# Four more pairs of projections in the seven-product part, and weights split ahead in the attention

## The chip, the cores and the metric

The kernel runs on one core of one Trainium2 chip. The metric is the device time of one execution in microseconds (us); of several executions the median is given. Work is spread over engines that run side by side, each through its own list of instructions in order: TensorE (PE, matmuls into PSUM), VectorE (DVE), ScalarE (ACT), GpSimd (POOL) and SyncE (SP), which here only issues DMAs. POOL issues some DMAs too. A DMA is issued when the instructions ahead of it in its queue are through and the buffers that it needs are free.

## The reference

Two layers on 512 latent and 256 context tokens of width 1024, in float32. The first mixes a long convolution (Hyena) and grouped-query attention; the second is an mLSTM with 8 heads, run over the tokens forwards and backwards. For the second layer the input `h` is projected to queries and keys of 128 columns a head and to values `v`, gates `o` and `z` of 256 columns a head:

```python
q, k, v, o, z, gates = _split(h @ w_in, ODD_SPLITS)
...
h = (h_f + h_b).transpose(0, 2, 1, 3).reshape(Bn, n, ML_WIDTH).astype(o.dtype) * jax.nn.sigmoid(o)
h = rms_norm(h.reshape(Bn, n, ML_HEADS, ML_V), head_norm.reshape(ML_HEADS, ML_V)).reshape(Bn, n, ML_WIDTH)
return (h * jax.nn.silu(z)) @ w_out
```

Keys and values are wanted for all 768 tokens, since the state starts from the context; queries, `o` and `z` for the 512 latent tokens alone.

## The kernel before

**Precision.** Every float32 operand is split into a rounded half `hi` and the rest `lo`: a copy with conversion on ACT and a subtract on DVE (`split`, line 1005). A product is then three matmuls, hi x hi, hi x lo and lo x hi (`mm3`, line 1015). A projection of one tile of 128 tokens on 256 columns goes over 8 blocks of the inner dimension, so it takes 24 matmuls of 256 columns (`proj_tok`, line 1202). The activations lie in SBUF as `hTh` and `hTl`.

**Weights.** `load_w` (line 1030) loads a slice of 1024 x 256 weights in two halves of 512 KB into one of three raw buffers `wr` (SP's queue) and splits each into `wh0`/`wl0` or `wh1`/`wl1`, two sets that take turns.

**Stages**, each recorded whole and then issued in an order that is written out in lists (`ORDERS`), which fix the sequence on every engine; `SLOTS` says which buffer each use of a tile gets:

- `start` and `hy`: norms, then the convolution in eight rounds `j`.
- `att`: 24 blocks `n` (8 heads by 3 groups of 256 queries). Scores (two PSUM tiles `s`), their maximum on DVE, the exponential on ACT into `hdh`/`hdl`, the scaling on DVE, transposes on PE, splits into `PTh`/`PTl`, and the products with the values (`values`, line 2006). Between them stand projections for the next heads. Behind block 19 the output projection begins, whose sums go into the tile `yacc0`; until then `yacc0` is unused. The query norms take a small power on POOL (`rstd`, line 1076; tile `rq`).
- `out0`: the rest of the first layer's output, and the second layer's input.
- `l1a`: values of head 0, the mLSTM's gate terms, keys and queries of head 0, and gates `o` and `z` of heads 0 to 6 by seven products.
- `l1b`: for each head `h` the recurrence in both directions (scores with `E`, the state `C` with its halves `Ch` and `Cl`, the sums `num`), interleaved with keys, queries and six value tiles of head `h + 1` (`heads`, line 2527). With the last head the work that stands between is `o` and `z` of head 7.
- `out1`: the second layer's output. Its first 96 matmuls already stand at the end of `l1b`.

**Seven products.** Two projections of the 512 latent tokens, `o` and `z` of a head, are taken as one product of 2 x 2 blocks: 256 tokens by 512 inner rows, times 512 inner rows by 256 columns of `o` or of `z`. A scheme of Strassen's kind needs seven block products instead of eight, each 24 matmuls: 168 for a pair. The sums of activations (`D1`, `F5`, `F6`, `F3`) are made once. The four sums of weight blocks for each pair are made in DRAM during the convolution: `oz_sums` (line 1635) issues, in each of the eight rounds, one copy (SP's queue) or one accumulating DMA (POOL's queue) for each of seven pairs, 512 KB each, into `osum`. In `gates_oz` (line 2484) a pair loads seven blocks of 512 KB (three through `wr`, four through the two buffers `ch`), splits them, and combines the products on DVE in seven operations of 512 columns; `o` and `z` then go through ACT and to DRAM, from where `l1b` loads them.

All instructions go through one helper, so each row of the profile has the same line, L1000; they are told apart by the tiles that they write and read.

Of the kernel before, what the change touches and what calls it, by code (L numbers as in the profile page):

```python
# [2777 lines left out]
```

## Time and profile before

| | |
|---|---|
| three executions | 1489.63, 1490.12, 1491.56 us, median 1490.12 |
| profiled execution | 1491.61 us, span 1489.8 us |
| granted TensorE clock, mean | 0.997 |
| busy share of PE, DVE, ACT, POOL | 98%, 70%, 51%, 6% |
| stage `hy`, to about 395 us | PE without a break |
| stage `att`, about 425 to 742 us | DVE about 69%, ACT about 48% busy between 395 and 715 us |
| stage `l1a`, about 870 to 1045 us | DVE 73%, ACT 61% busy |
| stage `l1b`, 1045 to 1390 us | DVE 75%, ACT 68% busy |

The stages run into each other by some us. A row of groups reads: line, engine, operation, tile written <- tiles read, shapes, count | busy us, mean ns of one | idle time of the engine ahead of them and what ended it. A row of a tile gives the least, middle and longest duration in ns, the first and the last start in us, and the shapes. A row of waits reads: who <- for whom, us in total, times, longest us. A row of DMA issues gives the queue, the count, the size of one and the median us from issue to landing. POOLq and SPq are the queues of POOL and SP.

### The profile page before, as it was taken

What the parts mean: (1) busy time and instruction counts of PE and PEld (TensorE: products, weight loads), DVE (VectorE), ACT (ScalarE), POOL (GpSimd) and SP (SyncE); (2) the same over time, 40 slices, a digit from 0 to 9 for tenths busy, and PEclk for the clock granted to TensorE, in tenths of its full rate; (3) what the DMA queues carried; (4) which work ended last, traced back from release to release, by engine and by line L of the source; (5) the groups of instructions that cost most, each with busy time, mean ns of one, the idle gap of its engine ahead of it and who ended that gap; (6) DMA issues with size and microseconds to landing.
All of it is one profiled execution on the core that took longest, in us unless ns stands there. A gap on an engine that the chain in (4) does not pass through costs nothing. (4 is left out here: it accounts for less than half of the span.)

```text
span 1489.8 us, 25927 instructions
## 1 busy us (share of the span) xinstructions
PE 1457.7 (98%) x10362; PEld 1339.3 (90%) x10362; DVE 1037.1 (70%) x1927; ACT 766.3 (51%) x1577; POOL 82.5 (6%) x125
## 2 busy tenths in 40 slices
...
GB/s 378 221 140 144 146 162 131 147 140 183 76 100 43 54 96 54 82 117 114 164 222 68 134 123 155 203 267 198 156 117 97 113 62 86 124 88 140 153 205 123
DMA packets 57353, 205.79 MB, mean 138 GB/s; under 512 B 7003, under 2 KB 8539, under 8 KB 54448
## 3 DMA queue, kind: packets, MB, share of 16 engines
...
q14 instruction: 40, 0.33, 0.1%
...
## 5 line engine op out<-in xcount | busy, mean ns | idle before, releaser
L1000 PE MATMUL pj<-wh,hTh 128*128 128x256 f32 (+2 forms) x1200 | 340.6, 290 | 0.8 <-ACT qjunk L1000 0.4
L1000 PE MATMUL pj<-wl,hTh 128*128 128x256 f32 (+2 forms) x1200 | 337.4, 287 | 0.3 <-DVE wl L1000 0.3
L1000 PE MATMUL pj<-wh,hTl 128*128 128x256 f32 (+2 forms) x1200 | 336.7, 288 | 0.0
L1000 PE MATMUL pj<-hTh,wh 128*128 128x512 f32 (+1 forms) x832 | 286.8, 346 | 0.4 <-DVE vl L1000 0.3
L1000 PE MATMUL pj<-hTl,wh 128*128 128x512 f32 (+1 forms) x832 | 285.4, 344 | 0.4 <-DVE hTl L1000 0.4
L1000 PE MATMUL pj<-hTh,wl 128*128 128x512 f32 (+1 forms) x832 | 285.5, 345 | 0.0
L1000 PEld LDWEIGHTS pj<-wh,hTh 128*128 128x128 f32 x1200 | 224.3, 189 | 6.2 <-issue 2.7
L1000 PEld LDWEIGHTS pj<-wl,hTh 128*128 128x128 f32 x1200 | 225.0, 189 | 2.9 <-DVE wl L1000 0.5
L1000 PEld LDWEIGHTS pj<-wh,hTl 128*128 128x128 f32 x1200 | 223.9, 189 | 3.5 <-issue 1.5
L1000 DVE TENSOR_TENSOR wl<-wr,wh 128x1024 fp32r<-128x1024 f32 (+1 forms) x142 | 171.4, 1213 | 63.9 <-ACT wh L1000 63.9
L1000 ACT CAST wh<-wr 128x1024 fp32r<-128x1024 f32 (+1 forms) x142 | 146.7, 1043 | 83.4 <-PE pj L1000 55.8
L1000 PEld LDWEIGHTS pj<-hTh,wh 128*128 128x128 f32 x832 | 156.6, 189 | 18.5 <-DVE vl L1000 1.1
L1000 PEld LDWEIGHTS pj<-hTl,wh 128*128 128x128 f32 x832 | 156.8, 189 | 17.9 <-DVE hTl L1000 0.7
L1000 PEld LDWEIGHTS pj<-hTh,wl 128*128 128x128 f32 x832 | 156.4, 188 | 18.0 <-DVE wl L1000 0.3
L1000 DVE TENSOR_TENSOR PTl<-pj,PTh 128x384 fp32r<-128x384 f32 (+1 forms) x80 | 41.1, 526 | 18.8 <-ACT PTh L1000 18.4
L1000 ACT CAST PTh<-pj 128x384 fp32r<-128x384 f32 (+1 forms) x80 | 35.6, 459 | 30.5 <-PE pj L1000 29.8
L1000 DVE TENSOR_TENSOR wl<-ch,wh 128x1024 fp32r<-128x1024 f32 x28 | 34.2, 1221 | 24.5 <-ACT wh L1000 24.4
L1000 DVE TENSOR_REDUCE mx<-s 128x1 f32<-128x768 f32 (+1 forms) x48 | 37.2, 775 | 11.4 <-PE s L1000 11.2
L1000 PE MATMUL pm<-Rh,dfa 128*128 128x256 f32 (+1 forms) x192 | 45.0, 305 | 0.0
L1000 DVE TENSOR_TENSOR med<-big 128x512 f32<-128x512 f32 (+1 forms) x48 | 40.4, 864 | 5.0 <-ACT big L1000 4.8
L1000 PE MATMUL s<-dfa,qTh 128*128 128x256 f32 (+1 forms) x160 | 42.8, 338 | 0.7 <-ACT hdh L1000 0.6
L1000 DVE SCALAR_TENSOR_TENSOR C<-C,apb,pj 128x258 f32<-128x258 f32 x64 | 30.8, 481 | 16.5 <-PE pj L1000 11.8
...
## 6 DMA issues: line engine op xcount, KB each, us to landing
wr<-in_e_w_in SPq DMA_DIRECT2D x52, 512.0 KB, 5.3
wr<-in_o_w_in SPq DMA_DIRECT2D x50, 512.0 KB, 5.2
o_sums<-in_o_w_in POOLq DMA_DIRECT2D x28, 512.0 KB, 7.1
ch<-o_sums SPq DMA_DIRECT2D x21, 512.0 KB, 4.9
wh<-in_w_mod SPq DMA_DIRECT2D x10, 1024.0 KB, 7.3
wl<-in_w_mod SPq DMA_DIRECT2D x9, 1024.0 KB, 7.6
wr<-in_e_w_out SPq DMA_DIRECT2D x16, 512.0 KB, 4.5
wr<-in_o_w_out SPq DMA_DIRECT2D x16, 512.0 KB, 4.6
```

Source lines behind the costliest of these rows:

```text
L1000: x = fn(*a, **k)
```

## The change

1. The seven-product part takes eleven pairs instead of seven. The four new ones stand first: values of heads 1 and 2, of 3 and 4, of 5 and 6, and gate `o` of head 7 with values of head 7. Only latent tokens are done that way. The values are split there and both halves go to DRAM; `l1b` loads them into `vh` and `vl` and projects only the two context tiles of each head. The sums in DRAM grow accordingly, from 7 to 11 DMAs a round.
2. In the attention, behind each block's product with the values, up to three pieces of weights are split ahead: keys and queries of heads 2 to 7 and values of heads 1 to 7, 52 pieces of 128 x 512 (256 KB). A piece is loaded on POOL's queue into one of three places in `yacc0`, cast on ACT, subtracted on DVE, and both halves are stored to DRAM on POOL's queue.
3. In `l1b` these weights are loaded as ready halves straight into `wh`/`wl`, 1 MB each, on SP's queue.
4. `out_gate` of head 7 is gone from `l1b`.
5. The lists of order and buffers are new for `att` and the stages behind it. In `hy` the sequence is the same but for the DMAs added.

```diff
-    osum = nc.dram_tensor("o_sums", [7, 4, P, 4, 256], F32).ap()
+    PAIRS = [(5, 9), (13, 17), (21, 25), (30, 29)] + [(4 * h + 2, 4 * h + 3) for h in range(7)]
+    osum = nc.dram_tensor("o_sums", [len(PAIRS), 4, P, 4, 256], F32).ap()
+    def pair_blocks(n):
+        a, b = (ow[x] for x in PAIRS[n])
+        return a[:, 0:4], b[:, 0:4], a[:, 4:8], b[:, 4:8]
...
+    wsd = nc.dram_tensor("w_scratch", [8, 2, 2, P, KT, 256], F32).ap()
+    ahead = [(h, t, k) for h in range(1, 8) for t in range(2) for k in range(0, KT, 2)][4:]
+    begun = []
+    def split_ahead():
+        if begun:
+            h, t, k, hi, lo = begun.pop()
+            S.copy(hi, f(lo))
+            V.tensor_tensor(lo, f(lo), f(hi), ALU.subtract)
+            for i, x in enumerate((hi, lo)):
+                G.dma_start(wsd[h, t, i][:, k:k + 2], f(x))
+        if ahead:
+            h, t, k = ahead.pop(0)
+            w = yacc0[:, 2 * (len(ahead) % 3):][:, :2].rearrange("p a (t b) -> p a t b", t=2)
+            hi, lo = w[:, 0].bitcast(F32R), w[:, 1].bitcast(F32R)
+            G.dma_start(f(lo), ow[4 * h + t][:, k:k + 2])
+            begun.append((h, t, k, hi, lo))
...
         values(n, PTh, PTl)
+        for _ in range(3):
+            split_ahead()
...
+    def load_split(h, t):
+        slot = wslot[0]
+        wslot[0] = 1 - slot
+        hi, lo = (wtile(f"w{x}{slot}", F32R) for x in "hl")
+        for i, x in enumerate((hi, lo)):
+            SP.dma_start(f(x), wsd[h, t, i])
+        return hi, lo
...
         def load(self):
-            self.w = w_next if self.h == 1 else load_w(ow[4 * self.h])
+            self.w = w_next if self.h == 1 else load_split(self.h, 0) if self.h else load_w(ow[0])
         def load_v(self):
-            self.wv = load_w(ow[4 * self.h + 1])
+            for t, src in ((self.vh, vd[self.h, 0]), (self.vl, vd[self.h, 1])):
+                SP.dma_start(f(t[:, 0:4, :256]), src)
+            self.wv = load_split(self.h, 1)
...
+        for x, c, kind in zip(PAIRS[n], (ca, cb), kinds):
+            if kind == "v":
+                hi = T(wp, "wr", (P, 4, 256), F32R, bufs=3).rearrange("p (t i) b -> p t (i b)", t=2)
+                S.copy(hi, c)
+                V.tensor_tensor(c.bitcast(F32R), c, f(hi), ALU.subtract)
+                dst = [(vd[x // 4, 0], f(hi)), (vd[x // 4, 1], c)]
+            else:
+                dst = [(ozd[x // 4, "oz".index(kind)], c)]
+            for d, t in dst:
+                SP.dma_start(d, t.rearrange("p t (i b) -> p (t i) b", b=256))
+    for n in range(len(PAIRS)):
+        pair_product(n)
...
-            work = [(N.key, 0), (N.key, 1), (N.query,)] + [(N.value, i) for i in (4, 5, 0)] + [(N.turned,)] + [(N.value, i) for i in (1, 2, 3)]
+            work = [(N.key, 0), (N.key, 1), (N.query,)] + [(N.value, i) for i in (4, 5)] + [(N.turned,)]
         else:
-            wo = load_w(ow[4 * h + 2])
+            SP.dma_start(so, ozd[h, 0])
             wz = load_w(ow[4 * h + 3])
...
-            work = [(out_gate, i) for i in range(4)] + [(gate_z, i) for i in range(4)]
+            work = [(gate_z, i) for i in range(4)]
```

`pair_product` is `gates_oz` with the two projections of a pair as its operands; what is between the products is unchanged.

More of the change, by code (lines that the diff above doesn't have):

```diff
@@ L729 @@
     "xt@0": [
-        1, 4, 3, 5, 0, 2, 4, 1, 3, 5, 2, 4,
+        3, 5, 4, 0, 2, 1, 5, 3, 4, 0, 1, 5,
     ],
     "wr@1": [
[4 rows of a table removed]
[3 rows of a table added]
     ],
@@ L741 @@
     "sst@0": [
-        0, 1, 4, 2, 3, 5,
+        0, 1, 2, 3, 4, 5,
     ],
     "rs@0": [
-        0, 1, 2, 3, 4, 5,
+        0, 1, 4, 3, 2, 5,
     ],
@@ L754 @@
     "pm@3": [
[4 rows of a table removed]
[4 rows of a table added]
     ],
     "g@4": [
-        0, 1, 0, 1, 0, 1, 0, 1,
+        1, 0, 1, 0, 1, 0, 1, 0,
     ],
     "x0s@4": [
-        0, 1, 0, 1, 0, 1, 0, 1,
+        1, 0, 1, 0, 1, 0, 1, 0,
     ],
@@ L769 @@
     "med@4": [
[3 rows of a table removed]
[3 rows of a table added]
     ],
     "big@4": [
-        0, 1, 0, 0, 1, 0, 0, 1, 0, 0, 1, 0, 0, 1, 0, 0, 1, 0, 0, 1, 0, 0, 1, 0,
+        1, 0, 1, 1, 0, 1, 1, 0, 1, 1, 0, 1, 1, 0, 1, 1, 0, 1, 1, 0, 1, 1, 0, 1,
     ],
     "rt@6": [
-        1, 0, 0, 1, 0, 1, 0, 0, 1, 1, 0, 1, 1, 0, 1, 0, 1, 1, 0, 1, 0, 1,
+        0, 1, 1, 1, 0, 1, 1, 0, 1, 0, 1, 0, 0, 0, 1, 0, 1, 1, 0, 1, 0, 1,
     ],
     "gs@6": [
-        0, 0, 1, 2, 0, 1, 2, 0, 1,
+        0, 0, 2, 1, 0, 2, 1, 0, 2,
     ],
     "qTl@6": [
-        0, 1, 0, 2, 1, 0, 2, 1, 0,
+        0, 2, 0, 1, 2, 0, 1, 2, 0,
     ],
     "qTh@6": [
-        0, 0, 1, 2, 0, 1, 2, 0, 1,
+        0, 0, 2, 1, 0, 2, 1, 0, 2,
     ],
@@ L802 @@
     "rq@6": [
-        2, 3, 0, 1, 2,
+        1, 2, 3, 0, 1,
     ],
     "s2@8": [
-        1, 0, 1, 0, 0, 1, 1, 0, 0, 1, 0, 1, 1, 1, 0, 1, 0, 1, 1, 0, 1, 0, 1, 1, 0, 1, 0, 1, 1, 0, 0, 1, 0, 0, 1, 1, 0, 0, 1, 0, 1, 0, 0, 1, 1, 0, 1,
+        0, 1, 1, 0, 1, 1, 0, 1, 1, 0, 1, 1, 0, 1, 0, 1, 0, 0, 1, 0, 1, 0, 1, 0, 0, 1, 0, 1, 0, 1, 1, 1, 0, 0, 1, 0, 0, 1, 1, 0, 1, 0, 1, 0, 1, 0, 1,
         0,
@@ L809 @@
     "mx@6": [
-        3, 2, 0, 1, 2, 3, 1, 0, 2, 3, 0, 1, 2, 3, 0, 2, 1, 3, 0, 2, 1, 3, 0, 2, 1, 3, 0, 2, 3, 1, 0, 2, 1, 0, 3, 1, 2, 3, 0, 2, 1, 3, 2, 0, 1, 3, 0,
-        2,
+        0, 3, 1, 2, 0, 3, 1, 2, 0, 3, 1, 0, 2, 3, 1, 0, 2, 3, 1, 0, 2, 3, 1, 0, 2, 3, 1, 0, 3, 2, 1, 0, 3, 2, 1, 0, 2, 3, 1, 0, 3, 2, 1, 0, 3, 2, 1,
+        0,
     ],
     "sm@6": [
-        3, 2, 1, 0, 2, 3, 0, 1, 2, 3, 1, 0, 3, 2, 1, 0, 3, 2, 1, 0, 3, 2, 1, 0, 3, 2, 1, 0, 2, 3, 1, 0, 3, 1, 2, 3, 0, 1, 2, 0, 3, 1, 0, 2, 1, 3, 0,
+        0, 3, 1, 2, 3, 0, 1, 2, 3, 0, 1, 2, 3, 0, 1, 2, 3, 0, 1, 2, 3, 0, 1, 2, 3, 0, 1, 2, 3, 0, 1, 2, 3, 0, 2, 1, 0, 3, 2, 1, 0, 3, 1, 2, 0, 3, 1,
         2,
@@ L823 @@
     "pj@10": [
[6 rows of a table removed]
[5 rows of a table added]
     ],
     "pm@11": [
[5 rows of a table removed]
[5 rows of a table added]
     ],
     "yraw@9": [
-        1, 1, 0, 0, 0, 1, 1, 1,
+        0, 0, 0, 0, 1, 1, 0, 0,
     ],
@@ L853 @@
     "xn@9": [
-        1, 0, 1, 2, 2, 0, 1, 2, 0, 1, 0, 2,
+        0, 1, 2, 0, 1, 2, 0, 2, 0, 1, 2, 1,
     ],
@@ L865 @@
     "ch@13": [
-        1, 0, 1, 0, 1, 0, 1, 0, 1, 0, 1, 0, 1, 0, 1, 0, 1, 0, 1, 0, 1, 0, 1, 0, 1, 0, 1, 0,
+        0, 1, 0, 0, 1, 1, 0, 1, 0, 1, 0, 1, 0, 1, 0, 1, 0, 1, 0, 1, 0, 1, 0, 1, 0, 1, 0, 1, 0, 1, 0, 1, 0, 1, 0, 1, 0, 1, 0, 1, 0, 1, 0, 1,
     ],
     "decay@14": [
-        0, 1, 0, 1, 1, 0, 0, 1, 1, 0, 1, 0, 0, 1, 1, 0,
+        1, 0, 1, 0, 1, 0, 1, 1, 0, 1, 0, 1, 0, 1, 0, 1,
     ],
     "C@14": [
-        0, 1, 0, 1, 0, 1, 0, 1, 0, 1, 0, 1, 0, 1, 0, 0, 1, 0, 1, 0, 1, 0, 1, 0, 1, 1, 0, 1, 0, 1, 1, 0, 1, 0, 1, 0, 1, 0, 1, 0, 1, 0, 1, 0, 1, 1, 0,
-        1, 0, 1, 1, 0, 1, 0, 1, 0, 1, 0, 1, 0, 1, 0, 1, 0, 1, 1, 0, 1, 0, 1, 0, 1, 0, 1, 0, 0, 1, 0, 1, 0,
+        1, 0, 1, 0, 1, 0, 1, 0, 1, 0, 1, 0, 1, 0, 1, 0, 1, 0, 1, 0, 0, 1, 0, 1, 0, 0, 1, 0, 1, 0, 1, 0, 1, 0, 1, 0, 1, 0, 1, 0, 1, 0, 1, 0, 1, 0, 1,
+        0, 1, 0, 1, 0, 1, 0, 1, 0, 1, 0, 1, 0, 0, 1, 0, 1, 0, 1, 0, 1, 0, 1, 0, 1, 0, 1, 0, 1, 0, 1, 0, 1,
     ],
     "Ch@14": [
-        0, 1, 0, 1, 0, 1, 1, 0, 0, 1, 1, 0, 0, 1, 0, 1, 0, 1, 0, 1, 1, 0, 1, 0, 1, 0, 1, 0, 1, 0, 1, 0, 0, 1, 1, 0, 1, 0, 1, 0, 1, 0, 1, 0, 1, 0, 1,
-        1, 1, 0, 1, 0, 1, 0, 1, 0, 1, 0, 0, 1, 1, 0, 1, 0,
+        1, 0, 1, 0, 1, 0, 0, 1, 0, 1, 0, 1, 0, 1, 1, 0, 0, 1, 1, 0, 0, 1, 0, 1, 0, 1, 0, 0, 1, 0, 1, 0, 0, 1, 1, 0, 1, 0, 1, 0, 1, 0, 1, 1, 0, 1, 1,
+        0, 0, 1, 1, 0, 1, 0, 1, 0, 0, 1, 0, 1, 0, 1, 1, 0,
     ],
     "Cl@14": [
-        0, 1, 0, 1, 0, 1, 0, 1, 1, 0, 1, 0, 0, 1, 0, 1, 0, 1, 1, 0, 0, 1, 1, 0, 1, 0, 1, 0, 1, 0, 1, 0, 0, 1, 0, 1, 0, 1, 1, 0, 1, 0, 1, 0, 1, 1, 0,
-        0, 1, 0, 1, 0, 1, 0, 1, 0, 1, 0, 0, 1, 1, 0, 1, 0,
+        0, 1, 0, 1, 1, 0, 0, 1, 0, 1, 0, 1, 0, 1, 1, 0, 0, 1, 1, 0, 0, 0, 1, 0, 1, 0, 1, 1, 0, 1, 0, 1, 0, 1, 0, 1, 0, 1, 0, 1, 0, 1, 0, 0, 1, 0, 0,
+        1, 0, 1, 1, 0, 1, 0, 1, 0, 0, 1, 0, 1, 0, 1, 0, 1,
     ],
     "dn@14": [
-        1, 0, 0, 2, 3, 2, 2, 1, 1, 0, 0, 3, 3, 2, 2, 1,
+        0, 1, 1, 2, 3, 2, 2, 0, 0, 1, 1, 3, 3, 2, 2, 0,
     ],
     "yraw2@15": [
-        0, 1, 2, 3, 0, 1, 2, 3,
+        0, 2, 2, 3, 3, 1, 0, 1,
     ],
@@ L892 @@
     "esst@15": [
-        0, 1, 0, 1,
+        1, 0, 1, 0,
     ],
     "ers@15": [
-        0, 1, 0, 1,
+        1, 0, 1, 0,
     ],
     "xt@15": [
-        2, 0, 1, 3,
+        1, 0, 3, 2,
     ],
@@ L1628, in _body, with pair_sums @@
     ow = ins["o_w_in"]
-    osum = nc.dram_tensor("o_sums", [7, 4, P, 4, 256], F32).ap()
-    def oz_blocks(h):
-        o, z = ow[4 * h + 2], ow[4 * h + 3]
-        return o[:, 0:4], z[:, 0:4], o[:, 4:8], z[:, 4:8]
-    def oz_sums(step):
-        for h in range(7):
-            b11, b12, b21, b22 = oz_blocks(h)
-            t = osum[h]
+    PAIRS = [(5, 9), (13, 17), (21, 25), (30, 29)] + [(4 * h + 2, 4 * h + 3) for h in range(7)]
[3 more added lines that the diff above has]
+        return a[:, 0:4], b[:, 0:4], a[:, 4:8], b[:, 4:8]
+    def pair_sums(step):
+        for n in range(len(PAIRS)):
+            b11, b12, b21, b22 = pair_blocks(n)
+            t = osum[n]
             dst, src, add = ((t[0], b12, 0), (t[2], b12, 0), (t[0], b11, 1), (t[2], b22, 1),
@@ L1697, in _body @@
         norms()
-        oz_sums(j)
+        pair_sums(j)
         def last(s, parts=parts, g=g, x0s=x0s, rn=rn, j=j):
@@ L2261, in _body @@
     ncd = nc.dram_tensor("nc_scratch", [2, 8, NL], F32).ap()
-    ozd = nc.dram_tensor("oz_scratch", [7, 2, P, 4, 256], F32).ap()
+    ozd = nc.dram_tensor("oz_scratch", [8, 2, P, 4, 256], F32).ap()
+    vd = nc.dram_tensor("v_scratch", [8, 2, P, 4, 256], F32).ap()
     g1 = ExitStack()
@@ L2482, in raw_block, with pair_product, done @@
         return raw
-    def gates_oz(h):
-        b11, b12, b21, b22 = oz_blocks(h)
-        t1, t2, t3, t4 = (osum[h, i] for i in range(4))
-        so = T(gp, "so", (P, 2, 512))
-        zs = T(gp, "zs", (P, 2, 512))
+    def pair_product(n):
+        b11, b12, b21, b22 = pair_blocks(n)
+        t1, t2, t3, t4 = (osum[n, i] for i in range(4))
+        ca = T(gp, "so", (P, 2, 512))
+        cb = T(gp, "zs", (P, 2, 512))
         uu = T(gp, "uu", (P, 2, 512))
         u, u2 = uu[:, 0], uu[:, 1]
+        kinds = [" voz"[x % 4] for x in PAIRS[n]]
         def summed(src):
             return weights(raw_block(src, "ch", 2, gp))
+        def done(t, kind):
+            if kind == "o":
+                S.activation(t, t, AF.Tanh, scale=0.5)
+            elif kind == "z":
+                S.activation(t, t, AF.Silu)
         p1 = product(PJ(), A11, summed(b11))
@@ L2497, in gates_oz @@
         p2 = product(PM(), A12, weights(raw_block(b21)))
-        V.tensor_tensor(so[:, 0], p2, u, ALU.add)
-        S.activation(so[:, 0], so[:, 0], AF.Tanh, scale=0.5)
+        V.tensor_tensor(ca[:, 0], p2, u, ALU.add)
+        done(ca[:, 0], kinds[0])
         q5 = product(PJ(), F5, summed(t1))
@@ L2503, in gates_oz @@
         V.tensor_tensor(u2, q6, u, ALU.subtract)
-        V.tensor_tensor(zs[:, 0], q5, u2, ALU.add)
+        V.tensor_tensor(cb[:, 0], q5, u2, ALU.add)
         V.tensor_tensor(u2, q7, u2, ALU.add)
-        V.tensor_tensor(zs[:, 1], q7, zs[:, 0], ALU.add)
-        S.activation(zs[:, 1], zs[:, 1], AF.Silu)
+        V.tensor_tensor(cb[:, 1], q7, cb[:, 0], ALU.add)
+        done(cb[:, 1], kinds[1])
         q3 = product(PM(), F3, weights(raw_block(b22)))
-        V.tensor_tensor(zs[:, 0], q3, zs[:, 0], ALU.add)
-        S.activation(zs[:, 0], zs[:, 0], AF.Silu)
+        V.tensor_tensor(cb[:, 0], q3, cb[:, 0], ALU.add)
+        done(cb[:, 0], kinds[1])
         q4 = product(PJ(), A22, summed(t4))
-        V.tensor_tensor(so[:, 1], q4, u2, ALU.subtract)
-        S.activation(so[:, 1], so[:, 1], AF.Tanh, scale=0.5)
-        SP.dma_start(ozd[h, 0], so.rearrange("p t (i b) -> p (t i) b", b=256))
-        SP.dma_start(ozd[h, 1], zs.rearrange("p t (i b) -> p (t i) b", b=256))
-    for h in range(7):
-        gates_oz(h)
-        if h == 1:
+        V.tensor_tensor(ca[:, 1], q4, u2, ALU.subtract)
+        done(ca[:, 1], kinds[0])
+        for x, c, kind in zip(PAIRS[n], (ca, cb), kinds):
[8 more added lines that the diff above has]
+                SP.dma_start(d, t.rearrange("p t (i b) -> p (t i) b", b=256))
+    for n in range(len(PAIRS)):
+        pair_product(n)
+        if n == 1:
             turn()
```

4 lines of the change are left out of this document (removed), and 1140 rows, old and new, of tables (ORDERS, SLOTS).

## The prediction

> **What bounds the kernel now.** I read the first part of the page, then the spacing of single matmuls in the timeline, then the busy times stage by stage, then who waits for whom on TensorE, and last the groups and tiles that price the moved work. The profiled execution took 1491.61 us around a span of 1489.8 us; the median of the runs shown is 1490.12 us, 1.5 us less. I sum against the profiled execution and then take off that 1.5 us.
>
> ```profile
> PE 1457.7 (98%) x10362; PEld 1339.3 (90%) x10362; DVE 1037.1 (70%) x1927; ACT 766.3 (51%) x1577; POOL 82.5 (6%) x125
> ```
>
> A busy PE says little by itself, since matmuls overlap: in the timeline one of 256 columns is drawn 0.28 us long, but the next one starts 0.12 us later.
>
> ```profile
> 1096.05 0.28 PE L1000 MATMUL pj<-hTh,wh 128*128 128x256 f32 x1
> 1096.17 0.28 PE L1000 MATMUL pj<-hTl,wh 128*128 128x256 f32 x1
> 1096.29 0.28 PE L1000 MATMUL pj<-hTh,wl 128*128 128x256 f32 x1
> ```
>
> The stages, each row giving stretch, length, then busy us (count) of PE, PEld, DVE, ACT, POOL, the clock, the DMA share and GB/s. The first is the recurrence with the projections of the next head, the second the layer's seven-product part, the third the attention, the fourth the long convolution:
>
> ```profile
> 1045.00:1390.00 345.00, 342.81 (x2539) 325.29 (x2538) 260.23 (x540) 235.07 (x579) 24.90 (x45) 1.00 0.33 105
> 870.00:1045.00 175.00, 173.03 (x1381) 169.99 (x1380) 127.83 (x172) 107.15 (x150) 0.00 (x0) 1.00 0.56 188
> 395.00:715.00 320.00, 315.54 (x2403) 294.30 (x2402) 219.58 (x505) 154.12 (x391) 16.86 (x13) 1.00 0.26 84
> 80.00:395.00 315.00, 315.00 (x1978) 284.55 (x1977) 249.26 (x407) 129.43 (x207) 20.32 (x25) 1.00 0.55 142
> ```
>
> In all four PE has work nearly all the time at full clock, and the longest sums that PE waited in the attention and in the recurrence are about 1 and 2 us:
>
> ```profile
> PE pj L1000 <- ACT qjunk L1000: 0.9, 3, 0.4
> PE pj L1000 <- DVE vl L1000: 2.1, 4, 1.1
> ```
>
> So PE's stream sets the time in each of these stages, and a matmul taken away is time taken away, as long as VectorE (DVE), ScalarE (ACT) and the DMAs keep PE fed.
>
> **Matmuls removed and added.** A projection of one 128-token tile on 256 columns is 8 x 3 = 24 matmuls. Values of heads 1 to 7 lose four of six tiles (7 x 4 x 24 = 672) and gate o of head 7 loses four (96): 768 leave the recurrence. Four pairs enter the seven-product part with 7 x 24 = 168 each: 672. Net, 96 fewer, all of 256 columns. Their price is read where nothing else runs on PE:
>
> ```profile
> 975.00:995.00 20.00, 20.00 (x170) 20.00 (x169) 12.64 (x14) 9.26 (x13) 0.00 (x0) 1.00 0.74 265
> ```
>
> 170 in 20 us is 0.118 us each, so **96 x 0.118 = 11.3 us** come off. The stages shift more: the recurrence loses 90 us (345 to 255), the seven-product part gains 79 us (175 to 254).
>
> **Recurrence: what leaves DVE and ACT, and what is left.** Rows for the splitting of weights and of values:
>
> ```profile
> L1000 DVE TENSOR_TENSOR wl<-wr,wh 128x1024 fp32r<-128x1024 f32 x141 | 171.0, 1219 | 63.9 <-ACT wh L1000 63.9
> L1000 ACT CAST wh<-wr 128x1024 fp32r<-128x1024 f32 x141 | 146.4, 1048 | 83.4 <-PE pj L1000 55.8 <-PE pm L1000 9.5 <-DMA wr<-in_e_w_out 5.9
> L1000 DVE TENSOR_TENSOR vl<-pj,vh 128x256 fp32r<-128x256 f32 x48 | 20.0, 420 | 9.9 <-ACT vh L1000 9.8
> L1000 ACT CAST vh<-pj 128x256 fp32r<-128x256 f32 x48 | 17.5, 367 | 13.9 <-PE pj L1000 11.2 <-DVE wa L1000 1.3 <-DVE hTl L1000 1.0
> ```
>
> 28 weight pieces go (keys and queries of heads 2 to 7: 12; values of heads 1 to 7: 14; gate o: 2) and 28 value tiles. DVE: 28 x 1.219 + 28 x 0.420 = 45.9 us less, 214 in 255 us, 84% where it was 75%. ACT: 28 x (1.048 + 0.367) = 39.6 us less, 195 in 255, 77% where it was 68%. PE leaves faster than its helpers do, so the stage becomes tighter. Rows for that density:
>
> ```profile
> 1325.00:1345.00 20.00, 20.00 (x171) 20.00 (x170) 15.78 (x35) 16.00 (x38) 0.64 (x1) 1.00 0.27 95
> 1345.00:1365.00 20.00, 19.59 (x162) 19.18 (x161) 13.77 (x30) 13.85 (x38) 1.01 (x1) 1.00 0.36 118
> 1365.00:1385.00 20.00, 20.00 (x169) 20.00 (x169) 16.86 (x39) 13.62 (x30) 0.00 (x0) 1.00 0.26 80
> 875.00:895.00 20.00, 18.72 (x118) 16.93 (x117) 18.70 (x27) 13.95 (x22) 0.00 (x0) 1.00 0.19 58
> 895.00:915.00 20.00, 19.30 (x146) 18.31 (x145) 19.35 (x35) 12.82 (x16) 0.00 (x0) 1.00 0.44 136
> ```
>
> At DVE 79 to 84% (15.78 and 16.86 of 20) PE loses nothing; at 93 to 97% it loses 1.28 and 0.70 us, 5% of 40 us. Bounds for 255 us: 0 and 12.6 us. The mean of 84% lies at the good rows, but the end does not: from 1345 to 1385 DVE works 30.6 us, the change takes 96 matmuls (11.3 us) of gate o out of there and only two splits (2.4 us) from DVE, which makes 28.2 us of DVE in 28.7 us. For those 30 us I take 5% and for the rest half a per cent: 1.5 + 1.1, say **+2.5 us**.
>
> The loads of that stage double: ready halves (2 MB instead of 1 MB) go straight into the weight buffers, so the next load waits until PE is done with the last user of the buffer, and it stands on SP's queue ahead of the decay rows and of the outputs. What has to fit is the landing of 1 MB:
>
> ```profile
> wh<-in_w_mod SPq DMA_DIRECT2D x10, 1024.0 KB, 7.3
> ```
>
> Two of those, one behind the other, are 15 us at worst. A head then takes 255/7 = 36 us. Its keys and queries, 24 matmuls of 256 columns and 48 of 512 at twice the price, hold their buffer for some 14 us: 22 us are left to refill it. Zero; if the cover were gone it would cost up to 13 x 15 us, which no row suggests.
>
> **Seven-product part.** Per added pair 7 weight pieces, 7 combinations of 512 columns; seven value blocks are split once more.
>
> ```profile
> L1000 DVE TENSOR_TENSOR zs<-pm,zs x14: 676/691/692, 920.0 to 1041.2; 128x512 f32<-128x512 f32 x14
> ```
>
> DVE gains 28 x 1.219 + 28 x 0.69 + 7 x 1.219 = 62 us and stands at 190 in 254 us, 75%, under the good rows. DMA: a pair of values moves 7 loads and 4 stores of 512 KB (5.8 MB) in 168 x 0.118 = 19.8 us, 291 GB/s where the row of 975 us shows 265 at a share of 0.74; so about 0.81 for 60 us. Zero, bounds -3 (more PE work lies beside the DVE crowd of 875 to 915 us, which now costs 2 us) to +3 (late loads).
>
> **Convolution stage: the sums.** 16 more copies and 16 more accumulations of 512 KB; the order list of the diff has otherwise the same sequence there, the new pairs spread evenly. 28 MB of sums become 44 MB. The stage moves 142 GB/s x 315 us = 44.7 MB; the 16.7 MB that are not sums would, at 265 GB/s per 0.74, take 0.15 of the share, so sums take 0.40 of the 0.55, and 44 MB take 0.63: 0.78 in all. PE ran without loss at 0.74. Zero, at most +3.
>
> **Attention: 52 pieces more.** Each has a load on POOL's queue, a cast on ACT, a subtract on DVE, two stores on POOL's queue. For 512 columns, SBUF to SBUF (the first two rows are from the tiles ql and qh), and for such a piece in this very stage (768 columns):
>
> ```profile
> L1000 DVE TENSOR_TENSOR ql<-cvo,qh x8: 660/684/685, 953.3 to 1330.9; 128x512 fp32r<-128x512 f32 x8
> L1000 ACT CAST qh<-cvo x8: 605/618/629, 946.8 to 1330.2; 128x512 fp32r<-128x512 f32 x8
> L1000 DVE TENSOR_TENSOR hTl<-dfb,hTh x4: 948/950/951, 681.8 to 695.8; 128x768 fp32r<-128x768 f32 x4
> 665.00:695.00 30.00, 29.93 (x237) 27.03 (x236) 26.86 (x60) 20.59 (x40) 2.20 (x3) 1.00 0.35 117
> ```
>
> DVE +35.6 us (255 of 320, 80%), ACT +32.1 us (186, 58%). Bounds: 0, and 35.6 us if every subtract lay on the path. The nearest row is 665 to 695 us, where eight such pieces run: DVE 90% busy, PE 29.93 of 30. Against it: the whole stage loses 4.5 us of PE now at 69%. I take two thirds of that again, **+3 us**.
>
> **POOL's rotation.** The pieces use three places in the yacc0 tile, so the load of piece k+3 waits on POOL's queue until both stores of piece k have landed, and behind it wait the next stores and the small power of the query norms, for which the scores wait. One turn, with prices for stores from SP and loads of other sizes, the nearest there are:
>
> ```profile
> L1000 POOL DMA_DIRECT2D cs<-y_scratch x2 | 1.5, 744 | 43.7 <-DVE shf L1000 43.7
> out_x<-xt SPq DMA_DIRECT2D x8, 256.0 KB, 2.0
> y_scratch<-dec SPq DMA_DIRECT2D x8, 384.0 KB, 4.5
> PTl<-in_rope POOLq DMA_DIRECT2D x1, 512.0 KB, 4.6
> cs<-y_scratch POOLq DMA_DIRECT2D x2, 768.0 KB, 5.4
> o_sums<-in_o_w_in POOLq DMA_DIRECT2D x28, 512.0 KB, 7.1
> ```
>
> Cast 0.62, subtract 0.68, two issues 1.49, store 2.0 to 4.5, load 4.6 to 5.4: 9.4 to 12.7 us; I take 11. What it may take: in the diff's order the 52 pieces go from entry 110 to entry 2544 of 3399, at 320 us some 229 us, 13.2 us for three. It fits by 2 us: zero extra.
>
> [...]
>
> [...]
>
> **The sum.** 1491.6 - 11.3 + 2.5 + 3 = 1485.8 for a profiled execution, less 1.5: **1484 us**.
>
> **Rivals.**
>
> *All of it hidden.* The 90% row and the 84% row both show PE full. Then 1490.1 - 11.3 = 1479 us. Against it: the small losses now, which more work on the helpers won't lessen.
>
> *The recurrence becomes DVE's.* Now E, the state C and its halves alternate between ACT and DVE at 84 and 77%. If the whole stage loses 4%, as the two rows before 915 us do, that is 10 us: 1490.1 - 11.3 + 10 + 3 = 1492 us or, at half of it, 1487: no change that can be told.
>
> *POOL's rotation runs late (slower).* From a turn of 13.2 us on, every further us costs 52/3 = 17 us of attention, for ACT and DVE work in order and the scores, the exponentials and the transposes stand behind the cast that waits. With the 7.1 us of an accumulation for the load and 4.5 for the store a turn is 0.62 + 0.68 + 1.49 + 4.5 + 7.1 = 14.4 us: +20 us, 1502 us; at 13.9 us it is +12, 1493 us. For it: margins of 2 us, a DMA share that rises from 0.26 (40 MB more in 229 us add 175 GB/s to 84). Against it: a load from DRAM into SBUF never took the 7.1 us, and PE loses the sum only where no slack is left.
>
> **How the numbers follow.** A measurement of this kernel can tell about 0.2%, 3 us, from no change: faster is under 1487.1, slower over 1493.1. Forecast around 1484 (1481 to 1487): 0.42. All hidden (1476 to 1481): 0.24. DVE-bound recurrence, within 0.2%: 0.15. Late rotation or that and a tight recurrence, over 1493: 0.19. So faster 0.66, same 0.15, slower 0.19. The range from 1477 to 1496 leaves out a tenth in the slow case and a little below.
>
> **What would show it.** Right: 10266 matmuls or so in all, the attention's stretch no more than 4 us longer, the stretch of the recurrence near 257 us with DVE at 83%, PE's waits for DVE there a few us. Wrong: ACT waiting for a DMA into yacc, by several us a time, with the attention 10 us or more longer (rotation); PE under 97% in the recurrence with DVE over 90% in its last 30 us (DVE-bound); weight splits in the convolution that wait for a late DMA (sums). If the time falls by more than 12 us, I have missed a gain outside the matmul count.

## The result, and the profile after

The change made the kernel slower: 1509.33 us (median of 6 runs, 1506.57 to 1513.6) against 1490.8 us before on the same chip, a ratio of 1.0126 with a 95% interval of 1.0109 to 1.0144. I had forecast 1484 us, 1477 to 1496: wrong in sign and outside the range. The profiled execution took 1511.4 us around a span of 1509.6 us, with a mean granted clock of 0.992 (0.997 before).

First the page's line of engines, for the kernel after:

```profile
PE 1459.5 (97%) x10266; PEld 1335.3 (88%) x10266; DVE 1079.8 (72%) x1986; ACT 788.6 (52%) x1608; POOL 179.9 (12%) x297
```

The 96 matmuls are gone (10362 to 10266), and the time went up. By stages of the kernel after (stretch, length, busy us and count of PE, PEld, DVE, ACT, POOL, clock, DMA share, GB/s): convolution, attention, seven-product part, recurrence, and the recurrence's last 20 us.

```profile
80.00:395.00 315.00, 315.00 (x1979) 284.59 (x1979) 249.21 (x406) 129.76 (x208) 31.69 (x39) 1.00 0.76 189
395.00:715.00 320.00, 304.01 (x2251) 281.02 (x2249) 237.80 (x527) 171.06 (x421) 103.42 (x170) 0.98 0.65 210
...
930.00:1145.00 215.00, 214.06 (x1787) 213.42 (x1786) 150.16 (x175) 113.56 (x145) 0.00 (x0) 1.00 0.72 241
1145.00:1400.00 255.00, 251.30 (x1745) 230.95 (x1744) 209.27 (x468) 194.04 (x510) 21.81 (x44) 1.00 0.63 221
1380.00:1400.00 20.00, 18.55 (x139) 16.92 (x138) 19.17 (x45) 17.60 (x48) 1.31 (x1) 1.00 0.19 67
```

Only the attention looks ill: in the same 320 us PE did 2251 matmuls where it did 2403. To put a number on each stage, I follow the starts of a few matmuls, the first or last with a certain tile, through both traces. Two rows of tile `f5h` (the activations of one of the seven products), before and after, show how it goes; the first start is the number to take:

```profile
L1000 PE MATMUL pj<-wh,f5h x56: 278/283/362, 906.1 to 1034.5; 128*128 128x256 f32 x56
```
```profile
L1006 PE MATMUL pj<-wh,f5h x88: 274/283/365, 928.1 to 1137.9; 128*128 128x256 f32 x88
```

| start of (us) | before | after | shift |
|---|---|---|---|
| first scores of the attention | 462.5 | 461.0 | -1.5 |
| last scores | 712.7 | 731.4 | +18.7 |
| first product with `f5h` | 906.1 | 928.1 | +22.0 |
| last of the seven products | 1040.9 | 1144.5 | |
| last product with `Eh` (recurrence) | 1381.2 | 1397.4 | +16.2 |
| end of the span | 1489.8 | 1509.6 | +19.8 |

Up to the attention's last scores 18.7 us are lost, and 3.3 more between there and the seven products. Of these 3.3, a longer stretch of low clock is a part: the granted clock is 0.67 and 0.50 in the two windows from 888 to 896 us, where the kernel before has 0.71 and 0.87 from 866 to 874. The stages from there on give back 2.2 us, not 11.3: the seven-product part grew by 81.6 us where 672 matmuls at 0.118 are 79.3 (+2.3); the recurrence shrank by 87.5 where 768 are 90.6 (+3.1); behind it 3.6 us were added.

In the attention the waits name the sign that the prediction had set down for a late rotation. Of the kernel after, who <- for whom, us in total, times, longest:

```profile
POOL yacc L1006 <- DMA w_scratch<-yacc: 66.9, 27, 10.4
...
ACT yacc L1006 <- DMA yacc<-in_o_w_in: 24.1, 14, 4.8
```

POOL waits for stores before it may issue the next load, and ACT waits 14 times for a load. But in the middle single operations and transfers last about what I had taken; rows of tile `yacc`, and the median from issue to landing:

```profile
L1006 POOL DMA_DIRECT2D w_scratch<-yacc x104: 539/539/869, 434.7 to 704.9; - x104
...
L1006 ACT CAST yacc<-yacc x52: 606/620/651, 432.7 to 676.1; 128x512 fp32r<-128x512 f32 x52
L1006 DVE TENSOR_TENSOR yacc<-yacc x52: 670/684/695, 433.7 to 682.2; 128x512 fp32r<-128x512 f32 x52
...
DMA to landing us min/median/max: 2.6/4.1/12.2
```
```profile
w_scratch<-yacc POOLq DMA_DIRECT2D x104, 256.0 KB, 4.0
...
yacc<-in_o_w_in POOLq DMA_DIRECT2D x52, 256.0 KB, 4.1
```

A median turn is 0.62 + 0.68 + 2 x 0.54 + 4.0 + 4.1 = 10.5 us, against 11 in the prediction and 13.2 on average available. The fault is in transfers that land late, and in what a missed turn costs. The chain of waits of the kernel after, near 480 us (start, us, what):

```profile
476.74 8.08 DMA yacc<-in_o_w_in
484.92 0.63 ACT yacc L1006
485.61 0.57 issue
486.18 0.68 DVE yacc L1006
486.86 0.48 DVE PTl L1006
487.39 2.29 PE pj L1006 x9
```

One load lands after 8.1 us; it is the last of six transfers that POOL's queue issued within 3.1 us, from 473.67 to 476.74, behind a power of the query norms. ACT stands at the cast, the splits of `PTh` and `PTl` stand behind the cast and the subtract, and PE, which needs them, starts no matmul for 3.4 us.

The second gap, of 3.7 us, ends at 577 us. Rows of SP's and POOL's queues in order of time (start, us, and in brackets the idle time and what ended it), then the chain:

```profile
556.90 0.42 SPq L1006 DMA_DIRECT2D wh<-in_w_mod  x1
557.37 0.47 SPq L1006 DMA_DIRECT2D wl<-in_w_mod  x1
...
571.00 1.15 POOL L1006 DMA_DIRECT2D yacc<-in_o_w_in  x2 [10.42 <-DMA w_scratch<-yacc]
```
```profile
558.96 11.76 DMA w_scratch<-yacc
570.72 0.28 issue
571.00 3.96 DMA yacc<-in_o_w_in
574.96 0.02 issue
574.98 0.63 ACT yacc L1006
```

The five transfers of pieces issued from 556.5 to 560.0 us took 7.2 to 12.2 us, 11.3 in the middle, beside two loads of 1 MB on SP's queue. So POOL's queue stood for 10.4 us, and the next load came too late. Pieces issued beside the same two loads are slow in the other runs as well: 8.4 to 10.5 us with the pieces alone, 7.9 and 8.0 with 26 pieces, 8.8 and 9.5 with 39. No run moves these loads, so that they are the cause is likely, but not shown.

What comes next is the surprise; windows of 4 us around both gaps:

```profile
484.00:488.00 4.00, 0.91 (x6) 0.70 (x5) 2.43 (x5) 2.88 (x6) 1.64 (x4) 0.82 0.35 141
488.00:492.00 4.00, 4.00 (x17) 3.71 (x17) 2.06 (x5) 1.47 (x3) 1.58 (x3) 0.50 0.76 230
492.00:496.00 4.00, 4.00 (x31) 4.00 (x30) 2.10 (x5) 3.04 (x5) 1.07 (x3) 0.82 0.26 86
574.00:578.00 4.00, 0.57 (x5) 0.56 (x5) 2.37 (x6) 2.40 (x4) 1.38 (x3) 1.00 0.48 193
578.00:582.00 4.00, 4.00 (x24) 4.00 (x23) 2.94 (x8) 1.81 (x5) 1.61 (x4) 0.59 0.85 292
```

Behind each gap PE is 100% busy at a lower granted clock, with 17 matmuls in the 4 us at 0.50; those of 256 columns start 0.21 us apart there (488.20, 488.41, 488.62 us), 0.12 at full clock. By the missing share of the clock, an estimate, a window at 0.50 loses 2.0 of its 4 us, one at 0.82 0.7, one at 0.59 1.6: 4.3 us on top of the 7.1 us of the two gaps. So behind gaps of 3.4 and 3.7 us the clock stood at 0.50 and 0.59. Of the gaps of 2.1 to 3.0 us in the runs below, some were followed by a lower clock too (last section).

### The profile page after: what moved, and what is told of

Same layout as the page of the kernel before. It is cut to its first block, busy times and chain, and to the rows that moved or that the text cites. A ratio compares the mean times of both kernels' runs of the same rounds, so it can differ in the third digit from the quotient of the medians.

```text
span 1509.6 us, 26392 instructions
## 1 busy us (share of the span) xinstructions
PE 1459.5 (97%) x10266; PEld 1335.3 (88%) x10266; DVE 1079.8 (72%) x1986; ACT 788.6 (52%) x1608; POOL 179.9 (12%) x297
## 4 chain that ended last, share of the span: by engine, by line
PE 73%; DVE 9%; DMA 7%; issue 4%; ACT 4%; POOL 2%; SPq 0%; POOLq 0%; DVEq 0%; ACTq 0%
PE pj L1006 54%; PE pm L1006 17%; DMA yacc<-in_o_w_in 3%; DMA w_scratch<-yacc 2%; DVE hh L1006 1%; PE s L1006 1%; DVE wl L1006 1%; POOL w_scratch L1006 1%; DMA oz_scratch<-so 1%; ACT wh L1006 1%; DVE yacc L1006 1%; DVE num L1006 1%; DVE cvo L1006 0%; ACT hf L1006 0%; DMA decay<-nc_scratch 0%
## 5 line engine op out<-in xcount | busy, mean ns | idle before, releaser
L1006 PE MATMUL pj<-wh,hTh 128*128 128x256 f32 (+2 forms) x1008 | 286.5, 291 | 1.8 <-ACT wh L1006 1.0
L1006 PE MATMUL pj<-wl,hTh 128*128 128x256 f32 (+2 forms) x1008 | 285.3, 290 | 2.0 <-DVE wl L1006 2.0
L1006 PE MATMUL pj<-wh,hTl 128*128 128x256 f32 (+2 forms) x1008 | 285.1, 290 | 0.0
L1006 PEld LDWEIGHTS pj<-wh,hTh 128*128 128x128 f32 x1008 | 189.3, 190 | 6.4 <-issue 1.6
L1006 PEld LDWEIGHTS pj<-wl,hTh 128*128 128x128 f32 x1008 | 189.8, 190 | 5.4 <-DVE wl L1006 2.6
L1006 PEld LDWEIGHTS pj<-wh,hTl 128*128 128x128 f32 x1008 | 189.4, 190 | 3.5 <-issue 1.7
L1006 PEld LDWEIGHTS pj<-hTh,wh 128*128 128x128 f32 x832 | 156.9, 189 | 19.8 <-issue 2.0
L1006 POOL DMA_DIRECT2D o_sums<-in_o_w_in x44 | 35.8, 819 | 322.6 <-DMA o_sums<-in_o_w_in 161.4
L1006 POOL DMA_DIRECT2D w_scratch<-yacc x104 | 56.8, 549 | 88.3 <-DVE yacc L1006 43.3
L1006 POOL TENSOR_SCALAR_AFFINE_SELECT decay<-decay 128x512 f32<-128x512 f32 x16 | 13.2, 829 | 410.9 <-DMA decay<-nc_scratch 384.1
L1006 ACT CAST wh<-ch 128x1024 fp32r<-128x1024 f32 x44 | 46.0, 1046 | 29.5 <-PE pj L1006 9.8
L1006 DVE TENSOR_TENSOR yacc<-yacc 128x512 fp32r<-128x512 f32 x52 | 35.5, 686 | 18.0 <-ACT yacc L1006 18.0
```

The lines of the kernel that those rows point to most:

```text
L1006: x = fn(*a, **k)
```

## The experiments

The first four take the attention apart, with the later stages left as before.

**The pieces alone, with the new order.** The kernel before, plus part 2 of the change and the new list for `att`; nobody reads what is stored.

```diff
+    def split_ahead(): ...
         values(n, PTh, PTl)
+        for _ in range(3):
+            split_ahead()
```

> The kernel before with the 52 pieces in the attention alone, in the order that the changed kernel has there; the halves in DRAM are read by nobody, the rest is as before. Theory rotation (the cast of piece k+3 stands in ACT's order before the two stores of piece k and the load behind them have landed, and the scores' work stands behind it): the attention is 18 to 22 us longer and the whole 1508 to 1513 us. If the 20 us came from the later stages or from their interplay with the attention: under 1497 us.

1509.7 us, 1.0125 [1.011, 1.014], the last scores 18.1 us later than before. So the attention alone, with the later stages as they were, makes a loss of this size, by the pieces or by their order.

**The order alone.** The new list with the 260 entries of the pieces taken out.

> The kernel before with the new order of the attention, but without any piece. Theory rotation: within 3 us of before, 1488 to 1494 us. Rival order (the new sequence itself is worse): 1500 us or more.

1491.0 us, 0.9999 [0.999, 1.0008]. The order costs nothing.

**Casts and subtracts alone.** No load, no store.

```diff
-            for i, x in enumerate((hi, lo)):
-                G.dma_start(wsd[h, t, i][:, k:k + 2], f(x))
...
-            G.dma_start(f(lo), ow[4 * h + t][:, k:k + 2])
```

> As e1, but the pieces have no DMAs: the 52 casts and subtracts work on yacc0, cleared once, in the same places of the order. Theory rotation: little, 1490 to 1496 us. Rival helpers (32 us more of ACT and 36 us more of DVE are what the attention can't hide): 1503 us or more.

1495.5 us, 1.0026 [1.0016, 1.0035]: +4.0 us, where the prediction had +3 for the 52 pieces on ACT and DVE.

**Loads and stores alone.** Cast and subtract left out, so the stores write the raw weights twice.

```diff
-            S.copy(hi, f(lo))
-            V.tensor_tensor(lo, f(lo), f(hi), ALU.subtract)
```

> As e1, but the pieces are only moved: each is loaded into its place and stored twice as it is, without cast and subtract; POOL's queue waits as it must, no other engine waits for it but for the norms' power. Theory rotation: 1489 to 1494 us. Rival traffic (40 MB more, or the norms' power stuck on POOL's queue): 1500 us or more.

1501.2 us, 1.0067 [1.0052, 1.0082]. A miss: transfers with no cast waiting for their data cost 9.7 us, more than the engine work. The trace has one long gap of PE, 4.5 us, that ends at 610 us. Two rows, of before and then of this run (start, us, engine, operation, tiles), show the power of the query norms that the scores there wait for:

```profile
598.15 2.27 POOL L1000 TENSOR_TENSOR rq<-qst,mhalf 128x12 f32<-128x12 f32 x1 [66.84 <-DVE sm L1000]
```
```profile
606.80 2.31 POOL L1008 TENSOR_TENSOR rq<-qst,mhalf 128x12 f32<-128x12 f32 x1
```

It starts 8.7 us later than before and 20.9 us behind its input, which the new list makes earlier (ready at 585.88 us; in the run with the order alone the power started at 582.52). It stands behind piece DMAs on POOL's queue that wait for stores to land, and DVE waited 4.8 us for it. The gap and the low clock behind it (0.75 and 0.82 in the windows from 608 to 616 us) make 4.5 + 1.0 + 0.7 = 6.2 of the 8.3 us by which this span is longer than before.

**The powers first.** Two runs move three of the five powers right behind their input, ahead of 5, 7 and 7 DMAs: in the kernel of transfers alone, and in the changed kernel.

```diff
   order list of att: three entries (rq) moved forward by 42, 37 and 102 places
   (in the changed kernel, whose list has more entries, by 48, 39 and 107)
```

> The kernel with the 52 loads and 104 stores alone took 1501.2 us, 9.7 over before, and its power of the query norms (rq) stood on POOL's queue behind piece DMAs that waited. Here three of the five rq of the attention are issued right behind the operation that makes their input, ahead of 5, 7 and 7 DMAs of pieces; nothing else is moved. Pieces are still neither cast nor subtracted (the stores write the raw weights twice), so the split is left out. Theory (the norms are late behind waiting DMAs): 1491 to 1494 us, no rq over 3 us after its input. Rival (the DMA traffic itself slows the loads of weights or the engines' access to SBUF): 1499 to 1502 us, unchanged.

1503.2 us, 1.0077 [1.006, 1.0094]: the expectation missed, though the mechanism stayed. The fourth power came at 600.96 us, 5.8 us earlier than in the run before, but still 18.7 us behind its input; the third was 8.5 us behind its own, and the fifth, which I hadn't moved, 18 us, all behind piece DMAs that waited for one another's landing. DVE waited for it:

```profile
DVE mx L1008 <- POOL rq L1008: 12.5, 2, 9.9
```

PE started no matmul for 8.4 us there: one gap in place of the other.

> The changed kernel with the same three rq moved ahead and nothing else. Theory (of the attention's 20 us some 8 are late norms, 4 the engine work, the rest ACT waiting for loads): 1500 to 1504 us. Rival (all of the loss is the rotation's waits on ACT, the norms' lateness only lies beside it): 1508 to 1511 us.

1516.2 us, 1.0174 [1.0158, 1.0189]: worse by 7 us, a clear miss. A power that stands ahead waits for its own input, and the loads behind it are late; the waits in this run:

```profile
ACT yacc L1007 <- DMA yacc<-in_o_w_in: 31.3, 15, 6.8
...
POOL rq L1007 <- DVE qst L1007: 23.8, 4, 13.0
```

Gaps of 6.3 and 4.3 us follow. On one queue in order, either the norms wait for the pieces or the pieces for the norms.

**The late power by itself.** To price it with no transfer added: the kernel before, the fourth power repeated over the same data.

```diff
             rstd(rq, self.ss, P, tmp, div)
+            normed.append(rq)
+            if len(normed) == 4:
+                for _ in range(3):      # 4 in the second run
+                    G.tensor_tensor(rq, tmp, mhalf[:, :12], ALU.pow)
```

> The kernel before with one power of the query norms (the fourth rq, at about 598 us) taken three more times on POOL over the same data, 2.29 us each: the scores wait 6.9 us longer for it, and nothing else is added, no DMA. In the kernel with the DMAs alone this rq was 8.7 us late, PE stood still for 4.4 us, so some 4.3 us are slack. Theory (a gap of about 3.4 us or more brings the granted clock down to half for some 4 us behind it): the gap is 2 to 3 us here, below that, and the time is 1493 to 1494 us with the clock at 1.00 behind it. Rival (a wait costs its length alone): the same here; the next run tells them apart. Third (the lateness of the norms was not what cost 9.7 us, the DMA traffic was): 1490 to 1492 us in both.

> The same with four more powers: 9.2 us late, a gap of 4.5 to 5 us. Theory (gap, and then half the clock for some 4 us): the gap and 3 to 4 us on top, 1498 to 1500 us, the granted clock at 0.5 to 0.6 in the 4 us behind the gap. Rival (a wait costs its length alone): 1495 to 1496 us, clock 1.00. Third (DMA traffic): 1490 to 1492 us.

1499.5 us, 1.006 [1.0043, 1.0077], and 1501.6 us, 1.0072 [1.0057, 1.0087]. The gaps were 5.5 and 7.9 us, 3 us longer than I had reckoned (there was less slack), so the first run did not stay below the 3.4 us of the expectation, the length of the first gap above, and the pair doesn't tell the theory from its rival by their difference. The clock does. Windows of the first run:

```profile
604.00:608.00 4.00, 0.00 (x0) 0.00 (x0) 0.47 (x2) 0.00 (x0) 3.42 (x2) 0.69 0.00 0
608.00:612.00 4.00, 3.94 (x19) 3.94 (x20) 0.17 (x2) 1.56 (x3) 0.00 (x0) 0.50 0.02 4
612.00:616.00 4.00, 4.00 (x25) 3.44 (x25) 3.15 (x8) 1.42 (x4) 0.00 (x0) 0.96 0.00 0
```

and of the second:

```profile
612.00:616.00 4.00, 4.00 (x19) 4.00 (x20) 0.18 (x2) 1.56 (x3) 0.00 (x0) 0.50 0.01 4
616.00:620.00 4.00, 4.00 (x19) 3.33 (x19) 3.06 (x7) 0.88 (x3) 0.00 (x0) 0.78 0.00 0
```

5.5 + 2.0 + 0.2 = 7.7 us for a span 7.3 longer, and 7.9 + 2.0 + 0.9 = 10.8 for one 10.3 longer. The third reading (the lateness of the norms costs nothing) would have left both at 1492 at most: it falls. With hardly a transfer running, one late power costs 8.8 and 10.9 us, as much as the 156 transfers did. That the transfers cost nothing besides isn't shown by these two runs.

**The pieces spread evenly.** The changed kernel with the attention's list of before, the pieces 5.1 us apart between 428 and 694 us in idle stretches of ACT and DVE, and each load 5 us behind the stores that free its place.

```diff
   order list of att: that of before, with the 52 pieces set in evenly; every rq right behind its input
```

> The changed kernel with the attention's order of before and the same 52 pieces spread evenly between 428 and 694 us (5.1 us apart, a turn of 15.3 us in place of an average of 13.2 with tight ones near 9), each cast and subtract in an idle stretch of its engine, each load planned 5 us behind the stores that free its place, each power of the query norms right behind its input on POOL's queue. Theory (the attention lost 18 to 20 us to a few gaps from late loads, and to the low clock behind them): no gap over 3 us, the attention 3 to 8 us longer than before, 1491 to 1496 us in all. Rival (the DMA traffic or the work on ACT and DVE costs the 18 us wherever it stands): 1505 to 1510 us.

1530.2 us, 1.0267 [1.0248, 1.0286], another miss. The last scores came 24 us later than before. In the attention gaps of 3.3, 2.1 and 4.5 us remained. For the first, three loads stood behind a power that waited for its input; for the last, a DMA into `cs` stood behind pieces, and ACT waited 5.4 us for it. A further gap, 8.8 us at 774 us, behind the attention, waits for weights of the next stage; the run below, which also joins the old attention list to the new lists behind it, has the same gap at 772 us, so it seems to come from that joining (not tried by itself). Only 3 of the 49 turns of this list are under 11 us (from its entries, as in the point-by-point account below), so roomier turns alone are no cure while three kinds of work share POOL's queue. Nor does this run speak against its rival, that the work costs the 18 us wherever it stands; the next two do.

**Fewer pieces.** The kernel before with the new order and every second piece, 26, or three of four, 39, at their places in the list. The places in `yacc0` come round every 26 or 17.6 us on average.

```diff
-    ahead = [... for k in range(0, KT, 2)][4:]
+    ahead = [... for k in range(0, KT, 2)][4::2]     # [4:43] for 39
```

> The kernel before with the attention's new order and every second piece only, 26 of 52, at the same places of the order; the three places in yacc0 then come round once in 26 us and not in 13, and each load is issued where it was, but the stores that it waits for are two pieces further back. The result doesn't use the pieces. Theory (the loss comes from turns that don't fit, which leave ACT waiting for a load and PE without work for over 3 us): no gap of PE over 2 us, ACT's waits for the loads under 5 us in all, half of the 4 us of the casts and subtracts and little else, 1491 to 1495 us. Rival (each piece costs its share, by traffic or by engine work): half of 18.7 us, 1499 to 1501 us.

> The kernel before with the new order of the attention and three pieces of four, 39, at their places: a turn is 17.6 us on average. Theory (a turn costs nothing until it doesn't fit, and the tight ones decide): 1493 to 1498 us, with one gap of PE over 3 us at most. Rival (the cost rises evenly from 26 pieces on): 1500 to 1501 us. Third (39 still fit): 1491 to 1493 us.

1492.0 us, 1.0009 [0.9999, 1.0019], and 1494.0 us, 1.0023 [1.0013, 1.0032]. The waits for loads, with 26 and then with 39 pieces:

```profile
ACT yacc L1007 <- DMA yacc<-in_o_w_in: 2.6, 3, 1.3
```
```profile
ACT yacc L1010 <- DMA yacc<-in_o_w_in: 6.9, 7, 1.8
```

No gap of PE over 1.2 us in either, though the slowest transfers of pieces still took 8.0 and 9.5 us; by the list the turns are 18.8 us and 12.1 us at least. Fewer pieces give longer turns and also fewer transfers side by side, and these runs don't tell the one from the other. So 26 pieces cost about 1 us, which can't be told from none, 39 cost 3, 52 cost 18: not a price per piece, but a point from which late transfers no longer fit into the turns. The last 13 pieces cost more than four times what the first 39 did.

**The later stages by themselves.** First with the old attention, and 26 copies of 1 MB from DRAM to DRAM in place of the pieces (both halves hold the raw weights; the splitting is left out).

> The changed kernel's seven-product part, recurrence and output, with the attention of before. In place of the pieces, 26 copies of 1 MB on POOL's queue fill the DRAM tensor, both halves with the raw weights, so the splitting of these weights is left out. Theory (the attention carries the loss and the later stages keep 6 of the 11.3 us): 1483 to 1488 us. Rival (the later stages gain all 11.3 us when they start undisturbed): 1479 to 1481 us; rival (they gain nothing): 1490 us or more.

1525.0 us, 1.023 [1.0214, 1.0245]: a bad stand-in. Beside the copies other transfers landed late; two rows of the chain of waits, for a store of 384 KB whose median before was 4.5 us:

```profile
548.04 17.40 DMA y_scratch<-dec
...
622.59 19.80 DMA y_scratch<-dec
```

So again, with the changed kernel and every second piece; the loads of ready halves take each piece twice.

```diff
-            SP.dma_start(f(x), wsd[h, t, i])
+            SP.dma_start(f(x).rearrange("p (a c b) n -> p a c (b n)", a=2, c=2),
+                         wsd[h, t, i].rearrange("p (a c b) n -> p a c (b n)", a=2, c=2)[:, :, 0:1].broadcast_to([P, 2, 2, 512]))
```

> The changed kernel with every second piece, as in the run before; each ready half is loaded in one transfer of 1 MB as before, whose source takes the piece that was split twice, so half of the splitting is left out and the second quarter and the fourth of these weights repeat the first and the third. Theory (the later stages lose most of the 11.3 us again: 2 in the seven-product part, 4 to 5 in the recurrence, 3.6 behind it): 1490.8 - 11.3 + 10 + 1 = 1488 to 1493 us. Rival (they lose it only because they start from a disturbed attention): 1480 to 1484 us.

1494.3 us, 1.0022 [1.0013, 1.0032], 1.3 us above the range expected. From the first `f5h` to the end this run gains 1.3 us on before (shift +4.9 there, +3.6 at the end), the changed kernel 2.2. So the later stages lose most of the 11.3 us with far less disturbance ahead of them. Even an attention that cost nothing would have left a gain of 1 or 2 us, less than the 3 us that the prediction took as the least that can be told. The recurrence in this run, and the same length before:

```profile
1130.00:1385.00 255.00, 247.89 (x1712) 227.23 (x1711) 207.17 (x464) 190.70 (x504) 20.39 (x44) 1.00 0.66 220
```
```profile
1128.00:1383.00 255.00, 252.81 (x1886) 240.31 (x1885) 191.19 (x399) 171.78 (x425) 17.25 (x29) 1.00 0.32 102
```

PE is without work for 7.1 us where it was for 2.2, with DVE at 81% in place of 75%. Why it is more than the 3.7 us of the changed kernel is open.

**The tail.** The changed kernel with the last stage's list of before.

```diff
   order list of out1: that of before
```

> The changed kernel with the order list of its last stage (the second layer's output) taken from the kernel before, nothing else. Its tail behind the recurrence was 3.6 us longer than before. Theory (the new list of that stage costs it): 1505 to 1507 us. Rival (what reaches that stage from the recurrence costs it): 1508.5 to 1510 us.

1507.1 us, 1.0114 [1.0096, 1.0133]: by its time the theory, but its trace says otherwise. From the last `Eh` to the end it takes 111.9 us, the changed kernel 112.2, before 108.6. The 2 us aren't clear of the noise: the interval overlaps that of the changed kernel (1.0109 to 1.0144). Its profiled execution was 6.1 us shorter, and 5.8 of these lie ahead of the tail: 1.7 up to the last scores, where the two gaps were 3.0 and 2.5 us, 1.8 between there and the seven products, 2.3 from there to the last `Eh`. At most 0.3 us of the tail are the list's.

## Why the prediction was wrong, point by point

The sum had 5.8 us less for the profiled execution (1491.6 to 1485.8); its span came out 19.8 longer. Of the 25.6 us between them, 15.7 arise up to the attention's last scores (18.7 where the sum had 3), 3.3 from there to the seven products, 2.3 in these, 0.6 in the recurrence and 3.6 behind it.

- **The matmuls, -11.3 us.** Right: 96 fewer.
- **Seven-product part, 0 (-3 to +3).** +2.3 us in the changed kernel, +0.9 in the run of it with half the pieces (80.2 us longer): inside the bounds. What stands ahead of it, behind the attention, had no term: +3.3 us. Convolution, 0: right; 315 us without a break at a DMA share of 0.76, where I had 0.78.
- **Recurrence, +2.5 us.** Mis-sized. DVE stood at 82% where I had worked out 84, and the place was right, the end: in the last 20 us DVE is 96% busy and PE loses 1.45 us. The loss was 3.1 us, and 7.0 in the run with half the pieces. I had reckoned 1% of the 255 us; the two traces show 1.5% (3.7 us without work) and 2.8%.
- **Behind the recurrence, no term.** +3.6 us: 0.9 from the last `Eh` to the last matmul, with 669 matmuls there where the trace before has 667, and 2.7 behind the last matmul (11.1 us for 8.4). Of these, 2.0 lie behind the issue of the last two stores of the output; their cause isn't settled.
- **Casts and subtracts, +3 us.** Right: +4.0 by themselves.
- **POOL's rotation, "It fits by 2 us: zero extra".** This step failed. The turn was right, 10.5 us for 11, but it is made of middle values and was held against a mean: it has no term for a transfer that lands late. The transfers of pieces landed after 2.6 to 12.2 us. Nor did it hold that "a load from DRAM into SBUF never took the 7.1 us": in the trace before, the loads into `wr` landed after up to 10.1 us, 5.2 in the middle. In the list the time from a piece's cast to the cast of the third after it runs from 84 to 250 entries, at 320 us for 3399 entries 7.9 to 23.5 us, and 15 of 49 are under 11 us. But these tight turns are not where most was lost: of the 24.1 us that ACT waited for loads, 5.9 lie on them. The two waits behind the large gaps, 4.8 and 4.5 us, lie on turns to which the list gives 12.4 and 17.6 us; they took 17.3 and 20.6, with the load of 8.1 us in the one and the stores of up to 12.2 us in the other. What waits for such a transfer at the head of POOL's queue holds up all that stands behind it, the loads of the next turns too.
- **The rival of the late rotation, 1493 to 1502 us.** It is what happened, and I gave it 0.19; 1509 us lies above it even so. Its mechanism was right (ACT and DVE in order, the splits of `PTh` behind the cast). Its price was not: I took 17 us for each us of the mean turn, and the middle turn was not late. Two gaps make most of it, in an estimate added up from this trace and the run with the casts and subtracts alone: 3.4 and 3.7 us, 4.3 us of low clock behind them, 4.0 us of casts and subtracts (a gap of 1.5 us among them), another gap of 1.6 us; together 17.0 of 18.7.
- **"the small power of the query norms, for which the scores wait".** I named it in that queue and gave it no price. Where it is late by 6.9 and 9.2 us it costs 8.8 and 10.9 us, as the runs with the power alone show. In the changed kernel the fourth came 9.9 us behind its input as well, but there it was not waited for: it was done at 612.13 us and first used 1.4 us later.

```profile
599.57 0.16 DVE L1006 TENSOR_SCALAR qst<-qss 128x12 f32<-128x12 f32 x1
...
609.65 2.48 POOL L1006 TENSOR_TENSOR rq<-qst,mhalf 128x12 f32<-128x12 f32 x1
...
613.56 0.21 DVE L1006 TENSOR_SCALAR mx<-mx,rq 128x1 f32<-128x1 f32 x1
```

DVE's waits for a power come to 1.8 us in this attention, in one piece. So little of the changed kernel's loss is a late power itself; the second power counts as work on POOL's queue ahead of the load of 8.1 us.

- **"two issues 1.49".** Over-priced: those of the stores took 0.54 us each in the middle and 0.87 at most, with DVE 74% busy (237.80 of 320 us).

Six places in place of three were not tried. Whether 52 pieces can be ordered so that every turn fits, late transfers included, stays open.
